# Beginning of a diffusion layer: lower halves of left blocks loaded in pairs, first high parts taken from PSUM, second tokens copied by two engines

## The chip, the cores and the metric

The kernel runs on one core of a Trainium2 chip. The metric is device time in microseconds (us) of one execution, lower is better; the figure given for a kernel is the median of several executions.

The core has five engines that run beside each other, each with its own queue of instructions in a fixed order: PE (TensorE, matrix products, with weight loads shown apart as PEld), DVE (VectorE), ACT (ScalarE), POOL (GpSimd) and SP (SyncE), which here only issues DMA transfers. They wait for each other through semaphores. Products are written to PSUM, a small memory that PE writes and that ACT and DVE read; everything else lies in SBUF, and inputs and outputs in HBM.

## The reference

One layer over 1024 latent tokens and 256 context tokens, width 1024, all in fp32: a SwiGLU FFN at half weight, a token mixer (gated short convolution beside grouped-query attention), a second FFN, and a final norm. Each part is normalised and modulated with a shift, a scale and a gate, made from the vector c.

```python
mod_lat = (jax.nn.silu(c) @ w_mod[layer] + b_mod[layer])[:, None, :]
ml = jnp.split(mod_lat, N_MOD, axis=-1)
x = x + 0.5 * ml[2] * swiglu(modulate(rms_norm(x, norm1_g), ml[0], ml[1]), ffn1_w_in, ffn1_w_out)
```

Only the start concerns us: the tokens x are read and normalised, `ml[1]` (scale) and `ml[0]` (shift) of the latents are made, and the first products of `ffn1_w_in` begin.

## The kernel before, in words

**Number format of the products.** An fp32 operand is split in two fp32r parts: a high part (a rounding cast) and a low part (the value minus the high part). A product is three matmuls: high by high, high by low, low by high. `split` does it with a cast on ACT and a subtraction on DVE.

**The products of the first FFN** go by a Winograd scheme (class `Winograd`): from the quarters of the weights and of the tokens seven products of half size are made for each of 22 column blocks, numbered 1 to 7 by the operand `r[i]` that they take. `r[1]` is the first half of the channels (0 to 511) of the first 512 tokens (C0), `r[2]` their second half (512 to 1023); `r[3]` to `r[7]` also need the second 512 tokens (C1). A product takes one left block (a weight tile of 128 by 512, in two parts) and is 12 matmuls of 128x512.

**The start by halves** (`start_by_half`, line 727). For the first `BY_HALF = 8` column blocks the products with `r[1]` are done first, which need only the upper halves of the blocks and the first half of the channels (left blocks 0 to 7; the first two products are interleaved). Then come the products with `r[2]`, with the lower halves (left blocks 8 to 15), each added by DVE to the result before. Five more column blocks follow with both products. `left()` keeps four left blocks ready: it draws from the generator `lefts` (line 618), which loads and splits. The upper halves come in pairs in tiles named `half`; each lower half has a buffer named `raw` to itself, of which there are three, each with room for two halves.

**What sets the order.** The instructions of each engine are ordered by a planner that plays the program through on modelled times: among the instructions that are ready it takes the one that stands earliest in the source, and it gives out the buffers of one kind in the source's order. Where the source says otherwise, an instruction is pinned: it comes after whatever stands just before it in the source for its engine. That is `pinned=True` for loads, matmuls and transposes, and `strict[0] = True` for all that is issued through `act`, `dve` and the others. The splits of the first 16 left blocks are pinned. The order is fixed before the run; on the chip an engine waits at an instruction whose inputs are late, and all behind it waits too.

**The modulation.** `first_mod` makes the first half of the scale (m = 1) on PE. `second_mod` (line 350) makes the others: DVE multiplies the rows of `w_mod` by silu(c) and sums them in `macc` (eight instructions, or four when `by_pe` is 4), the sum is split (`acch`, `accl`), PE adds over the partitions with a column of ones, ACT copies the row (`mrow`), PE turns it into a column, and DVE adds the bias into `modl`. `mod00` is the first half of the shift (m = 0); `mods1` is the second half of the scale, then of the shift, and its steps are drawn four at a time between the products of `start_by_half`.

**The tokens.** C0's tokens are scaled by their reciprocal norm (`scale_tokens`), then turned by PE (four transposes of 128x128 into a PSUM tile). The turned first half stays in four PSUM tiles `xh` until gain and shift are there; then `h0` is made (DVE for even k, ACT for odd k) and split by `keep` into `r[1]`. The second half is turned into `h0[k][:, 1]` once the first products are on their way, and later scaled, shifted and split into `r[2]`. C1's tokens are first turned unscaled by `turn_tokens` (eight times four transposes, one copy each; copies are for the residual), then scaled in place, and turned again in `norm1`, which makes `r[3]` to `r[7]` with sums and splits on DVE and ACT. `turn_tokens` takes PSUM tiles `pt` (two buffers) for even k and `po` (one buffer) for odd k.

Of the kernel before, what the change touches and what calls it, by code (L numbers as in the profile page):

```python
# [51 lines left out]
def tile_dit_layer(  # L52
# [56 lines left out]
    def uniq(s):  # L109
        n_tiles[0] += 1  # L110
        return f"{s}_{n_tiles[0]}"
# [238 lines left out]
    def second_mod(m, half, raws, by_pe=0):  # L350


        acc, nk = ttile("macc"), KD - by_pe
        for k in range(nk):
            raw, s = raws[k // 2][:, k % 2], silu_c[:, k : k + 1]
            if k:
                dve.scalar_tensor_tensor(out=acc, in0=raw, scalar=s, in1=acc, op0=ALU.mult, op1=ALU.add)
            else:
                dve.tensor_scalar(out=acc, in0=raw, scalar1=s, scalar2=None, op0=ALU.mult)
            yield  # L360
        ah, al = ttile("acch", dt=F32R), ttile("accl", dt=F32R)
        split(acc, ah, al)
        yield
        pr = ps_s()
        for k in range(nk, KD):
            raw, s = raws[k // 2][:, k % 2], silu_c[:, k : k + 1]
            matmul(pr[:1], s, raw, start=k == nk, stop=False, pinned=True)
            if k in (nk, KD - 1):
                yield
        matmul(pr[:1], ones_r[:], ah, start=not by_pe, stop=False)  # L370
        matmul(pr[:1], ones_r[:], al, start=False, stop=True)
        row = ttile("mrow")
        act.copy(out=row[:1], in_=pr[:1])
        yield
        pm = ps_t(4)
        for j in range(4):
            transpose(pm[:, j : j + 1], row[:1, j * P : (j + 1) * P])
        column_adds(m, half, pm, (0,))
        yield

# [111 lines left out]
    class Winograd:  # L492
# [21 lines left out]
        def keep(self, i, k, src, lo_eng=None):  # L514
# [3 lines left out]
            self.r[i][k] = t  # L518

        def modulated(self, out, k, ch, pr):  # L520
            dve.tensor_mul(out=out, in0=self.xs(k, ch), in1=pr)
            self.shifted(out, k)
# [95 lines left out]
        def lefts(self, pairs, side_from):  # L618
# [5 lines left out]

            def half_cols(src, half):
                t = wpool.tile([P, SLOT], F32, tag="raw", name=uniq("raw"), bufs=3)[:, :512]
                src = src[half * 512 : (half + 1) * 512]
                load(t.rearrange("p (k n) -> p k n", n=P), src.rearrange("(k p) n -> p k n", p=P))
                return t

# [11 lines left out]
            for t in self.halves[:m]:  # L642
                yield parts(t)
            for a, _ in pairs[:m]:
                yield parts(half_cols(a, 1))
            for a, _ in pairs[m:n]:
# [375 lines left out]

    def turn_tokens(ch, toks, engines=("dve", "act")):

        s, o, n = ch
        for k in range(KD):
            pt = (ps_o if k % 2 else ps_t)(n)
            for j, t in enumerate(toks):
                transpose(pt[:, j * P : (j + 1) * P], t[:, k * P : (k + 1) * P])
            dst = (xc if s == "c" else xs)(k, ch)  # L1030
# [54 lines left out]
    half1.h0 = h0 = [atile("h0", (P, 2, 512)) for _ in range(4)]  # L1085
    run(mod00, 1)
    half1.prefetch(2)
    run(mod00)
    for k in range(4):
        if k % 2:  # L1090
            half1.shifted(h0[k][:, 0], k, xh[k])
        else:
            dve.tensor_scalar(
                out=h0[k][:, 0], in0=xh[k], scalar1=gain1["l"][:, k : k + 1], scalar2=modl[:, k : k + 1],
                op0=ALU.mult, op1=ALU.add,
            )
        half1.keep(1, k, h0[k][:, 0])
    start = half1.start_by_half()
    run(start, 1)
    for k in range(4):  # L1100
        xt = turned(t0, k + 4, ps_o if k % 2 else ps_t)
        if k % 2:
# [3 lines left out]
    mods1 = (step for m, raws in ((1, raws11), (0, raws01)) for step in second_mod(m, 1, raws))  # L1106
    turn1 = turn_tokens(C1, t1, ("act", "act"))
    for j in range(2, BY_HALF):
        run(start, 1)
        run(mods1, 4)  # L1110
        if j == TOKENS_AT:
# [6 lines left out]
            run(turn1)  # L1118
            scale_tokens(t1, y1)
    run(mods1)  # L1120
# [780 lines left out]
```

## Time and profile before

| | us |
|---|---|
| median of 3 executions (lowest, highest) | 2656.81 (2656.78, 2657.75) |
| the profiled execution's own time | 2655.43 |
| its span, from the first instruction to the last | 2653.7 |
| PE busy | 2618.7 (99% of the span) |
| DVE busy | 2012.7 (76%) |
| ACT busy | 1172.7 (44%) |

The profile is of one execution. A time in a row is counted from the start of the span. A row of the order of time gives start, duration (of several: from the first's start to the last's end), engine, operation, out<-in with buffer numbers left out, and shapes; in square brackets stand the idle time of the engine before it and what ended it. The granted clock is the share of TensorE's full clock that PE was given. Names in rows: `ps`, `pt` and `po` are PSUM tiles, `wl` and `wh` the tiles of split left blocks (both hold a high and a low part), `r` the split token operands, `nt` the sums in `norm1`, `xtok` the tokens as loaded, `x` the turned tokens, `uc` the results of the start by halves.

### The profile page before, as it was taken

What the parts mean: (1) busy time and instruction counts of PE and PEld (TensorE: products, weight loads), DVE (VectorE), ACT (ScalarE), POOL (GpSimd) and SP (SyncE); (2) the same over time, 40 slices, a digit from 0 to 9 for tenths busy, and PEclk for the clock granted to TensorE, in tenths of its full rate; (3) what the DMA queues carried; (4) which work ended last, traced back from release to release, by engine and by line L of the source; (5) the groups of instructions that cost most, each with busy time, mean ns of one, the idle gap of its engine ahead of it and who ended that gap; (6) DMA issues with size and microseconds to landing.
All of it is one profiled execution on the core that took longest, in us unless ns stands there. A gap on an engine that the chain in (4) does not pass through costs nothing.

```text
span 2653.7 us, 35378 instructions
## 1 busy us (share of the span) xinstructions
PE 2618.7 (99%) x12665; PEld 2178.3 (82%) x12665; DVE 2012.7 (76%) x3382; ACT 1172.7 (44%) x2321; POOL 552.7 (21%) x425
## 2 busy tenths in 40 slices
PE   8999999999999999999999999999999999999998
PEld 5788799888788778888888888888887788888888
DVE  5778976887897899877798676685457876666996
ACT  6533354333454642333355576574235333334553
POOL 0143201112010044333023122141001442321100
PEclk9999999999999999999999999999999999999999
DMA  8556475344984355332522432113535552327831
GB/s 318 199 186 202 131 234 159 116 128 169 322 199 112 122 177 162 118 121 90 187 84 92 91 93 64 33 43 98 166 88 172 182 162 83 100 76 275 201 84 64
DMA packets 367017, 378.40 MB, mean 143 GB/s; under 512 B 19430, under 2 KB 252024, under 8 KB 366840
## 3 DMA queue, kind: packets, MB, share of 16 engines
q1 hardware_dynamic: 357400, 357.22, 41.7%
q0 software_dynamic: 9440, 18.91, 4.4%
q8 instruction: 99, 1.62, 0.3%
q14 instruction: 78, 0.64, 0.1%
HBM read 306.26 MB, written 69.76 MB: 142 GB/s over the span
## 4 chain that ended last, share of the span: by engine, by line
PE 85%; DVE 8%; DMA 2%; issue 2%; ACT 2%; POOL 0%; SPq 0%; DVEq 0%; ACTq 0%; POOLq 0%
PE ps L90 70%; PE po L90 8%; PE pt L90 7%; DVE wl L90 1%; DMA rawm<-in_w_mod_dram 1%; DVE u L90 1%; DVE macc L90 1%; DVE r L90 1%; DMA raw<-in_ffn_w_in_dram 1%; POOL sum L90 0%; DVE nt L90 0%; DVE y L90 0%; DVE xb L90 0%; DVE v L90 0%; DVE rs_t L90 0%
## 5 line engine op out<-in xcount | busy, mean ns | idle before, releaser
L90 PE MATMUL ps<-r,wl 128*128 128x512 f32 x5196 | 1208.7, 392 | 11.4 <-DVE wl L90 3.8
L90 PEld LDWEIGHTS ps<-r,wl 128*128 128x128 f32 x5196 | 974.9, 189 | 221.1 <-DVE wl L90 5.5
L90 ACT CAST wl<-raw 128x512 fp32r<-128x512 f32 x287 | 177.8, 620 | 222.4 <-PE ps L90 176.3
L90 ACT CAST wl<-sum 128x512 fp32r<-128x512 f32 x218 | 133.6, 620 | 305.9 <-PE ps L90 222.8
L90 DVE TENSOR_TENSOR wl<-raw,wl 128x512 fp32r<-128x512 f32 x287 | 204.3, 714 | 64.2 <-ACT wl L90 62.4
L90 DVE TENSOR_TENSOR wl<-sum,wl 128x512 fp32r<-128x512 f32 x218 | 198.3, 911 | 36.1 <-ACT wl L90 35.0
L90 POOL TENSOR_TENSOR sum<-raw 128x512 f32<-128x512 f32 x55 | 80.6, 1465 | 673.3 <-DMA raw<-in_ffn_w_in_dram 454.9
L90 DVE TENSOR_TENSOR u<-u,ps 128x512 f32<-128x512 f32 x186 | 126.3, 680 | 37.3 <-PE ps L90 37.3
L90 DVE SCALAR_TENSOR_TENSOR macc<-rawm,silu_c,macc 128x512 f32<-128x512 f32 x178 | 144.1, 827 | 13.4 <-DMA rawm<-in_w_mod_dram 12.9
L90 POOL TENSOR_TENSOR sum<-raw,sum 128x512 f32<-128x512 f32 x55 | 80.5, 1464 | 309.3 <-DVE wl L90 309.3
L90 ACT CAST rh<-hid 128x512 fp32r<-128x512 f32 x132 | 81.5, 621 | 136.5 <-PE ps L90 111.4
L90 DVE TENSOR_TENSOR pts<-pt,pts 128x512 fp32r<-128x512 f32 x160 | 108.8, 687 | 42.5 <-ACT pts L90 40.6
L90 ACT CAST pts<-pt 128x512 fp32r<-128x512 f32 x160 | 93.5, 595 | 86.4 <-PE pt L90 82.5
L90 DVE TENSOR_REDUCE m<-ps 128x1 f32<-128x512 f32 (+1 forms) x192 | 110.3, 595 | 23.9 <-PE ps L90 21.1
L90 PE MATMUL ps<-rh,wl 128*128 128x512 f32 x360 | 122.0, 389 | 0.0
L90 PE MATMUL ps<-wh,r 128*128 128x512 f32 x384 | 120.7, 392 | 0.0
L90 ACT CAST wh<-raw 128x512 fp32r<-128x512 f32 (+1 forms) x85 | 67.8, 801 | 101.9 <-PE ps L90 73.8
L90 DVE TENSOR_TENSOR rl<-hid,rh 128x512 fp32r<-128x512 f32 x132 | 90.4, 687 | 26.7 <-ACT rh L90 16.0
L90 PE MATMUL po<-pts,vh 128*128 128x512 f32 x256 | 110.0, 435 | 0.2 <-ACT pts L90 0.2
L90 PE MATMUL ps<-kl,qs 128*128 128x512 f32 x384 | 104.1, 395 | 0.0
L90 PE MATMUL ps<-rh,wh 128*128 128x512 f32 x300 | 102.3, 389 | 0.0
L90 PE MATMUL ps<-y,wc 128*128 128x512 f32 x384 | 97.1, 392 | 0.2 <-DVE g L90 0.2
(318 smaller groups left out, 5075.6 us busy)
## 6 DMA issues: line engine op xcount, KB each, us to landing
raw<-in_ffn_w_in_dram SPq DMA_DIRECT2D x130, 512.0 KB
raw<-in_ffn_w_out_dram SPq DMA_DIRECT2D x72, 512.0 KB
raw<-in_w_in_dram SPq DMA_DIRECT2D x61, 512.0 KB
rawm<-in_w_mod_dram SPq DMA_DIRECT2D x104, 256.0 KB
hid<-hd SPq DMA_DIRECT2D x40, 512.0 KB
rawm<-in_w_mod_dram SPq DMA_DIRECT2D x32, 512.0 KB
ucd<-uc SPq DMA_DIRECT2D x29, 512.0 KB
ws<-in_ffn_w_out_dram POOLq DMA_DIRECT2D x26, 512.0 KB, 6.4
```

The lines of the kernel that those rows point to most:

```text
L90: inst = getattr(self.engine, name)(*args, **kw)
```

## The change

1. **Modulation.** In `second_mod` the eight `macc` instructions of the scale's second half are pinned. For `mod00` the row copy and the add into `modl` are pinned, and the first two left blocks are drawn before `mod00`'s last two steps instead of between them; so their splits now stand before that row copy and that add.
2. **First token operand.** All instructions that make `h0`'s first half and `r[1]` are pinned. For even k the high part is no longer cast from `h0`: ACT computes it from the turned tokens in PSUM (`keep_turned`), with the same gain and shift; DVE still makes `h0` from the same PSUM tile and subtracts. The transposes of the second half are pinned, after the first two products.
3. **Lower halves.** Two lower halves go to one `raw` buffer, by two loads (`lower_halves`); left blocks 8 to 15 take four buffers instead of eight.
4. **Second tokens.** Of the eight copies of C1's turned tokens DVE takes those of odd k; before, ACT took all. Of the four tiles that are scaled in place ACT takes two; before, DVE took all.

```diff
@@ second_mod
+            strict[0] = not by_pe and m == 1
             if k:
                 dve.scalar_tensor_tensor(out=acc, in0=raw, scalar=s, in1=acc, op0=ALU.mult, op1=ALU.add)
             else:
                 dve.tensor_scalar(out=acc, in0=raw, scalar1=s, scalar2=None, op0=ALU.mult)
+            strict[0] = False
...
+        strict[0] = bool(by_pe)
         act.copy(out=row[:1], in_=pr[:1])
+        strict[0] = False
...
+        strict[0] = bool(by_pe)
         column_adds(m, half, pm, (0,))
+        strict[0] = False
@@ class Winograd
+        def keep_turned(self, i, k, turned, h):
+
+            t = atile(f"r{i}", (P, 2, 512), F32R)
+            self.shifted(t[:, 0], k, turned)
+            dve.tensor_sub(out=t[:, 1], in0=h, in1=t[:, 0].bitcast(F32))
+            self.r[i][k] = t
@@ lefts
-            def half_cols(src, half):
-                t = wpool.tile([P, SLOT], F32, tag="raw", name=uniq("raw"), bufs=3)[:, :512]
-                src = src[half * 512 : (half + 1) * 512]
-                load(t.rearrange("p (k n) -> p k n", n=P), src.rearrange("(k p) n -> p k n", p=P))
-                return t
+            def lower_halves(*srcs):
+                t = wpool.tile([P, 2, 512], F32, tag="raw", name=uniq("raw"), bufs=3)
+                for i, src in enumerate(srcs):
+                    load(t[:, i].rearrange("p (k n) -> p k n", n=P), src[512:].rearrange("(k p) n -> p k n", p=P))
+                return t[:, 0], t[:, 1]
...
-            for a, _ in pairs[:m]:
-                yield parts(half_cols(a, 1))
+            for j in range(0, m, 2):
+                yield from map(parts, lower_halves(pairs[j][0], pairs[j + 1][0]))
@@ the beginning
-    run(mod00, 1)
     half1.prefetch(2)
     run(mod00)
+    strict[0] = True
     for k in range(4):
         if k % 2:
             half1.shifted(h0[k][:, 0], k, xh[k])
+            half1.keep(1, k, h0[k][:, 0])
         else:
             dve.tensor_scalar(
...
-        half1.keep(1, k, h0[k][:, 0])
+            half1.keep_turned(1, k, xh[k], h0[k][:, 0])
+    strict[0] = False
...
-        xt = turned(t0, k + 4, ps_o if k % 2 else ps_t)
+        xt = turned(t0, k + 4, ps_o if k % 2 else ps_t, True)
...
-    turn1 = turn_tokens(C1, t1, ("act", "act"))
+    turn1 = turn_tokens(C1, t1, ("act", "dve"))
...
-            scale_tokens(t1, y1)
+            scale_tokens(t1, y1, True)
```

More of the change, by code (lines that the diff above doesn't have):

```diff
@@ L1021, in turned, with turn_tokens @@
         return pt
-    def turn_tokens(ch, toks, engines=("dve", "act")):
+    def turn_tokens(ch, toks, engines=("dve", "act"), pinned=False):
         s, o, n = ch
@@ L1028, in turn_tokens @@
             for j, t in enumerate(toks):
-                transpose(pt[:, j * P : (j + 1) * P], t[:, k * P : (k + 1) * P])
+                transpose(pt[:, j * P : (j + 1) * P], t[:, k * P : (k + 1) * P], pinned)
             dst = (xc if s == "c" else xs)(k, ch)
```

## The prediction

> **What bounds the kernel now.** I read the page first (its span), then the busy times by stretches of the beginning, then who waited for whom on PE up to 150 us, then the order of time on each engine around the waits. The change touches only work issued before about 110 us, so the stretches of the beginning count. In them the columns are busy us (instructions) of PE, PEld, DVE, ACT, POOL, then the granted clock, the DMA share and GB/s.
>
> ```profile
> span 2653.7 us, 35378 instructions
> 0.00:10.00 10.00, 6.38 (x36) 6.12 (x36) 0.24 (x2) 6.32 (x10) 0.71 (x6) 1.00 0.70 254
> 10.00:20.00 10.00, 9.79 (x44) 4.30 (x45) 6.43 (x20) 5.53 (x10) 0.00 (x0) 1.00 1.06 401
> 20.00:30.00 10.00, 8.38 (x41) 3.60 (x39) 6.00 (x14) 2.86 (x6) 0.00 (x0) 1.00 1.09 371
> 30.00:40.00 10.00, 8.90 (x38) 7.12 (x39) 9.96 (x16) 5.35 (x10) 0.00 (x0) 0.83 1.03 352
> 60.00:70.00 10.00, 7.52 (x38) 5.53 (x36) 6.87 (x14) 10.00 (x19) 0.00 (x0) 0.83 0.54 197
> 80.00:90.00 10.00, 10.00 (x54) 8.27 (x53) 10.00 (x18) 7.18 (x12) 0.00 (x0) 1.00 0.72 250
> 90.00:100.00 10.00, 7.71 (x29) 6.04 (x28) 9.98 (x18) 6.79 (x13) 0.00 (x0) 0.83 0.56 188
> ```
>
> PE is the bound nearly everywhere, except in three places: around 30, 63 and 91 us. In each it first waits, then runs with a granted clock of 0.83 over ten us, that is 1.7 us of full-speed work lost on top of the wait. The waits themselves, PE up to 150 us (total us, times, longest):
>
> ```profile
> PE ps L90 <- ACT wh L90: 2.3, 1, 2.3
> PE pt L90 <- ACT mrow L90: 1.4, 2, 0.7
> PE ps L90 <- ACT r L90: 1.3, 1, 1.3
> PE pt L90 <- DVE xtok L90: 1.2, 4, 0.5
> PE po L90 <- ACT x L90: 0.6, 1, 0.6
> PE pt L90 <- DVE h L90: 0.5, 1, 0.5
> ```
>
> Place 1 has half of the mrow wait, r and h: 0.7 + 1.3 + 0.5 = 2.5 us. Place 2 has the other half, xtok and x: 0.7 + 1.2 + 0.6 = 2.5 us. Place 3 is one wait of 2.3 us. With 1.7 us each for the clock, 7.3 + 5.1 = **12.4 us** is all that this change can reach; it will not clear three places at once.
>
> **The change part by part.** *Start of the first product (place 1).*
>
> ```profile
> 27.35 0.57 ACT L90 COPY mrow<-ps 1x512 f32<-1x512 f32 x1 [2.69 <-PE ps L90]
> 27.84 0.61 ACT L90 CAST wl<-half 128x512 fp32r<-128x512 f32 x1
> 28.42 0.16 DVE L90 TENSOR_TENSOR modl<-pt,bcol 128x4 f32<-128x4 f32 x1 [1.47 <-PE pt L90]
> 28.50 0.69 DVE L90 TENSOR_TENSOR wl<-half,wl 128x512 fp32r<-128x512 f32 x1
> 29.11 0.81 DVE L90 TENSOR_SCALAR h<-ps,gain_l,modl 128x512 f32<-128x512 f32 x1
> 29.95 0.62 ACT L90 CAST r<-h 128x512 fp32r<-128x512 f32 x1 [0.98 <-DVE h L90]
> 30.43 0.75 DVE L90 SCALAR_TENSOR_TENSOR macc<-rawm,silu_c,macc 128x512 f32<-128x512 f32 x1
> 30.47 0.77 ACT L90 ACTIVATE h<-ps,modl,gain_l 128x512 f32<-128x512 f32 x1
> 30.62 0.50 PE L90 MATMUL ps<-r,wl 128*128 128x512 f32 x1 [1.33 <-ACT r L90]
> 31.70 0.68 DVE L90 TENSOR_TENSOR r<-h,r 128x512 fp32r<-128x512 f32 x1
> 36.80 0.68 DVE L90 TENSOR_TENSOR r<-h,r 128x512 fp32r<-128x512 f32 x1
> ```
>
> Moved: the first two weights' casts and low parts now come before the mrow copy and the column add, into the 2.69 and 1.47 us in which ACT and DVE stood idle. So h starts where the low part started, 28.50 instead of 29.11. Added: h's high part goes from PSUM by ACT, 0.77 (the 30.47 row) instead of the cast's 0.62. No row shows ACT and DVE reading one PSUM tile side by side with neither needing the other. Bounds: side by side, the high part ends at 28.5 + 0.8 = 29.3 and PE starts 1.3 earlier; one after the other, it starts 0.84 after h (29.95 − 29.11), at 29.34, ends at 30.1, and PE starts at 30.15, 0.5 earlier. I take the second, as in the nearest row both engines read one PSUM tile and DVE's idle time is ended by ACT:
>
> ```profile
> L90 DVE TENSOR_TENSOR pts<-pt,pts 128x512 fp32r<-128x512 f32 x160 | 108.8, 687 | 42.5 <-ACT pts L90 40.6
> ```
>
> The Trainium skill speaks here against the change: "PSUM — Partial Sum Buffer", on bank collisions, says that two engines may not touch the same bank and partitions at once, two reads included, and that the compiler's scheduler puts a dependency between them. By it the sum is the one I took, 0.5; without it 1.3. No run here shows it yet.
>
> The low parts follow in written order with no macc (0.75, the 30.43 row) or copy between. From 30.15: low part 0 0.6; h 1 and its cast on ACT in 1.3, low part 1 0.6, ending at 32.0; h 2 and its high part one after the other 1.6, low part 2 beside h 3 and its cast 1.3, low part 3 0.7: 35.6. Before, low part 3 ended at 36.80 + 0.68 = 37.5. That is 1.9 earlier. Against it, the second half's 16 transposes are pinned behind the first 24 matmuls and no longer fill the waits; four take 0.44 on the chain, so 1.8 us come back later. And PE has even less to do up to 32 us, so the slow clock stays. Net: 0.5 us earlier, bounds −0.3 and 1.3.
>
> *Loads.*
>
> ```profile
> 12.71 4.56 SPq L90 DMA_DIRECT2D raw<-in_ffn_w_in_dram  x3
> 17.31 3.25 SPq L90 DMA_DIRECT2D half<-in_ffn_w_in_dram  x2
> ```
>
> Three raw buffers now take six loads, and up to three more may stand ahead of the first halves. What SP issued up to the halves is about 7.7 MB (4 + 8 loads of 0.52, 5 of 0.26, small ones); at 2.54 MB in the first ten us, 4.01 in the next and 371 GB/s after, the halves land by about 23. Three more (0.79 MB) make that 25.2, and the casts are done by 26.5 to 27, just ahead of 27.35. Cost 0, covered by that slack; without it the mrow copy queues behind them (bound 0.5 us). The gain of raw data earlier is judged at place 3.
>
> *Second half of the modulation, second tokens (place 2).*
>
> ```profile
> 47.19 0.48 DVE L90 TENSOR_SCALAR macc<-rawm,silu_c 128x512 f32<-128x512 f32 x1
> 48.65 0.57 ACT L90 COPY mrow<-ps 1x512 f32<-1x512 f32 x1
> 50.38 3.11 DVE L90 SCALAR_TENSOR_TENSOR macc<-rawm,silu_c,macc 128x512 f32<-128x512 f32 x4
> 59.66 0.61 ACT L90 COPY x<-po 128x512 f32<-128x512 f32 x1
> 62.53 2.93 ACT L90 ACTIVATE h<-h,modl,gain_l 128x512 f32<-128x512 f32 x4
> 63.04 2.74 DVE L90 TENSOR_SCALAR xtok<-xtok,rs_y 128x1024 f32<-128x1024 f32 x4 [0.72 <-PE po L90]
> 16.84 2.19 ACT L90 ACTIVATE xtok<-xtok,rs_y 128x1024 f32<-128x1024 f32 x2 [1.10 <-DVE rs_y L90]
> 67.03 0.78 PE L90 MATMUL ps<-r,wl 128*128 128x512 f32 x1
> 44.32 0.69 DVE L90 TENSOR_TENSOR wl<-half,wl 128x512 fp32r<-128x512 f32 x1 [1.33 <-ACT wl L90]
> ```
>
> Place 2 ends when r2 is there, and that hangs on the chain macc, mrow, modl, h. The scale's eight macc were spread over DVE's gaps from 25 to 40 us; now four are pinned behind the low parts of weights 4 and 5 and four behind that of weight 6, which was 44.32 and still follows product 2. So they end no sooner than 45.0 + 4 × 0.78 = 48.1; cast 0.6, low part 0.7 and two row matmuls 0.8 put the first mrow at 50.2, against 48.65. The shift's eight macc begin around that copy (47.19 before), so **1.6 us later**, or 3.5 if PE takes a whole product (2.7) first. From 47.19 to 62.53 are 15.3 us, of which the chain's own work is 0.5 + 7 × 0.75, 0.6, 0.7, 0.8, 0.6 and about 0.6 for turn and add: 8.5. The other 7 are queues, mostly ACT's, which is full (10.00 in 60 to 70). There four of the eight copies (0.6 each, 2.4) go to DVE, and two scalings (2.19) come, but only when all turns are done, so partly while ACT waits for this chain. I put the relief at 1.6, which cancels the delay: product(2) begins at **67.0**, bounds 64.5 and 70. The 0.5 of the start only lengthens this wait.
>
> *Place 3.*
>
> ```profile
> 88.04 0.62 ACT L90 CAST wl<-raw 128x512 fp32r<-128x512 f32 x1 [1.65 <-DMA raw<-in_ffn_w_in_dram]
> 91.53 0.62 ACT L90 CAST r<-nt 128x512 fp32r<-128x512 f32 x1 [0.16 <-DVE nt L90]
> 92.05 0.61 ACT L90 CAST wh<-raw 128x512 fp32r<-128x512 f32 x1
> ```
>
> PE waits for the cast at 92.05, the last of the lower halves. It is not late for its data: it is pinned behind the cast at 91.53, that one came right after DVE's nt, and DVE is full (10.00 and 9.98). Raw data loaded earlier takes the 1.65 us at 88.04 away, but that idle time stands beside a full DVE: worth 0. What helps is DVE: scaling on it falls from 2.74 to 1.4, the scaled tokens are ready some us sooner, and nt and r work can start in the 3.1 us in which DVE stood idle from 60 to 70. I put the cast 1 to 3 us earlier, and of 2.3 + 1.7 at this place I take half, **2.0** (bounds 0 and 4.0).
>
> **Sum:** 0 + 0 + 0 − 2.0, from the profiled execution's own 2655.43 (its span of 2653.7 and 1.7 around it): 2653.4. The median shown is 1.4 above that execution, so **2654.8** by the median, 0.08% less. What this kernel's times can tell from no change is put at 0.2%, 5.3 us.
>
> **The rivals.** *B, two places clear:* the high part is read side by side, ACT's relief beats the pins, product(2) begins 2.5 earlier and place 3 goes whole (4.0): 2656.8 − 6.5 = **2650.3**. For it speaks that ACT has not a gap from 60 to 70; against it, that the pins delay the chain ahead of ACT. The clock could add to it: the rows give 0.83 after waits of which the longest are 1.3, 0.7 and 2.3. The Trainium skill, "TensorE: Matmul & The Clock Gate", Part 1, has half rate only after a whole idle window of some 3.4 us; by that rule shortened waits would surely keep the clock and I would give B 0.4. The rows show the slow clock after shorter waits, so the trace does not agree. *C, hidden:* DVE stays the bound of place 3 whatever comes earlier, and nothing else shows: **2656.8**. For it: 9.98 and 10.00. *D, slower, a new wait in place 2:* the row matmuls of the scale slip behind one more product (2.7), y1's steps and four copies compete with the shift's macc on DVE, and r2 comes at 71.2, 4.2 later, with place 3 as before: **2661.0**. It decides from the point where the shift's first macc begins after 52 us. Against it: DVE had 3.1 us free in 60 to 70.
>
> **How the numbers follow.** Forecast 0.43 (2652 to 2657), B 0.27, C 0.15, D 0.15. Range 2648.5 to 2661: B's with the clock of one more place kept (1.7) to D's; about 0.1 lies below and 0.08 above. Faster by over 5.3 us (below 2651.5): most of B and a little of the forecast, 0.27. Slower by over 5.3 (above 2662.1): the part of D in which two products slip ahead, 0.07. The rest, 0.66.
>
> **What would show it.** Start: h about 0.6 earlier; ACT's high part beginning after DVE's h (my sum) or with it (B). Loads: no idle time of ACT before the mrow copy that a half's DMA ends. Place 2: first macc of the shift at 49 to 51, product(2) near 67. Place 3: PE's wait there under 2.3 us with DVE full. I am wrong if product(2) moves by more than 3 us, if place 3's cast waits for its load, or if the stretches after 130 us change by more than 1 us in sum.

## The result, and the profile after

The changed kernel is **slower**: 2672.73 us (median of 6 runs, 2671.22 to 2673.9) against 2656.8 for the kernel before beside it (6 runs, 2651.17 to 2657.97), ratio 1.0063 [1.0053, 1.0073]. 2654.8 was forecast, so the time missed is some 18 us. The profiled execution took 2672.8 us.

First the stretches of the profile after, columns as in the prediction: busy us (instructions) of PE, PEld, DVE, ACT and POOL, granted clock, DMA share, GB/s.

```profile
30.00:40.00 10.00, 9.37 (x35) 7.61 (x36) 5.02 (x8) 6.06 (x10) 0.00 (x0) 0.71 1.08 369
...
50.00:60.00 10.00, 5.15 (x16) 3.84 (x15) 7.46 (x11) 1.21 (x2) 0.00 (x0) 0.66 0.36 138
...
70.00:80.00 10.00, 5.17 (x27) 3.41 (x27) 5.71 (x17) 8.08 (x13) 0.00 (x0) 0.83 0.38 147
...
100.00:110.00 10.00, 7.15 (x31) 5.59 (x30) 10.00 (x18) 6.08 (x11) 0.00 (x0) 0.87 0.51 191
...
130.00:2600.00 2470.00, 2453.80 (x11731) 2041.07 (x11730) 1881.59 (x3113) 1078.20 (x2150) 545.37 (x417) 1.00 0.46 139
```

The same view of the kernel before, where its rows are not yet shown:

```profile
50.00:60.00 10.00, 10.00 (x58) 8.08 (x58) 7.74 (x21) 8.20 (x16) 0.00 (x0) 1.00 0.51 176
...
130.00:2590.00 2460.00, 2443.66 (x11698) 2034.79 (x11697) 1883.56 (x3107) 1074.76 (x2143) 541.35 (x411) 1.00 0.46 138
```

After 130 us nothing changed: PE stands still for 16.2 us of 2470 there, and for 16.3 of 2460 before. All is lost in the beginning, and the largest part of it in a stretch that before had no gap at all: 50 to 60 us, where PE is now busy for 5.15 us, at 0.66 of its clock. If the work lost in ten us is taken as ten less busy time times clock, the stretches up to 130 us add up to 15.4 us before and 29.3 after. The 13.9 more lie thus: 1.6 from 0 to 40 us, 6.9 from 40 to 60, 4.8 from 60 to 90, 0.6 from 90 to 130. This is rough, since the clock is a mean over each row; the spans, 2671.0 and 2653.7, differ by 17.3.

Who PE waited for from 20 to 150 us after the change (total us, times, longest):

```profile
PE ps L90 <- ACT acch L90: 4.8, 1, 4.8
PE ps L90 <- ACT wh L90: 2.9, 1, 2.9
```

The greatest wait is new: PE waits for `acch`, the high part of the scale's sum. The order of time on PE, ACT and DVE shows how it comes about and what it leaves behind (start, duration, engine, operation, out<-in, idle time before and what ended it):

```profile
44.94 0.60 PE L90 MATMUL po<-ident,xtok 128*128 128x128 f32 x4
45.57 0.59 ACT L90 COPY h<-po 128x512 f32<-128x512 f32 x1 [2.12 <-PE po L90]
46.71 0.69 DVE L90 TENSOR_TENSOR wl<-half,wl 128x512 fp32r<-128x512 f32 x1 [5.47 <-ACT wl L90]
47.92 0.48 DVE L90 TENSOR_SCALAR macc<-rawm,silu_c 128x512 f32<-128x512 f32 x1
51.28 3.11 DVE L90 SCALAR_TENSOR_TENSOR macc<-rawm,silu_c,macc 128x512 f32<-128x512 f32 x4
54.42 0.62 ACT L90 CAST acch<-macc 128x512 fp32r<-128x512 f32 x1 [3.77 <-DVE macc L90]
55.09 0.59 PE L90 MATMUL ps<-acch,ones_r 128*1 128x512 f32 x1 [4.85 <-ACT acch L90]
55.48 4.85 PE L90 MATMUL ps<-r,wh 128*128 128x512 f32 x12
55.68 0.48 DVE L90 TENSOR_SCALAR macc<-rawm,silu_c 128x512 f32<-128x512 f32 x1
61.77 0.40 PE L90 MATMUL ps<-accl,ones_r 128*1 128x512 f32 x1
63.14 0.56 ACT L90 COPY mrow<-ps 1x512 f32<-1x512 f32 x1
63.60 0.61 ACT L90 CAST wl<-raw 128x512 fp32r<-128x512 f32 x1
64.25 0.69 DVE L90 TENSOR_TENSOR wl<-raw,wl 128x512 fp32r<-128x512 f32 x1 [6.51 <-ACT wl L90]
80.00 0.80 PE L90 MATMUL ps<-r,wl 128*128 128x512 f32 x1 [0.59 <-ACT r L90]
```

The same view of the kernel before, for the same steps:

```profile
39.95 0.59 ACT L90 COPY h<-po 128x512 f32<-128x512 f32 x1 [2.68 <-PE po L90]
41.09 0.69 DVE L90 TENSOR_TENSOR wl<-half,wl 128x512 fp32r<-128x512 f32 x1 [0.95 <-ACT wl L90]
41.48 0.62 ACT L90 CAST acch<-macc 128x512 fp32r<-128x512 f32 x1
47.97 0.40 PE L90 MATMUL ps<-acch,ones_r 128*1 128x512 f32 x1
```

It is a ring of three engines, each with a fixed order. The last four transposes for the first tokens stand behind products on PE (44.94). ACT waits for them to copy `h`, with the cast of the next weight, at 46.05, behind that copy. DVE waits 5.47 us for that cast, and the pinned `macc` stand behind its low part. So the scale's sum begins at 47.92, where before its high part had been ready since 42.1, 5.9 us ahead of its use at 47.97. Now PE's order has come to the sum's first row matmul long before the sum is there: it waits 4.85 us, and the next 12 matmuls take 4.85 us, 0.40 each instead of 0.23.

A second round follows. The order has the low part's row matmul 19 matmuls behind the high part's, so on the slow clock it comes at 61.77. ACT copies the row at 63.14 (48.65 before), with the cast of the first whole weight behind it, and DVE waits 6.51 us for that cast, in the middle of the shift's sum. The shift is late, and with it `r[2]`: product(2) starts at 80.00 instead of 67.03.

### The profile page after: what moved, and what is told of

It is laid out like the page before. It is cut to its first block, busy times and chain, and to the rows that moved or that the text cites. A ratio compares the mean times of both kernels' runs of the same rounds, so it can differ in the third digit from the quotient of the medians.

```text
span 2671.0 us, 35369 instructions
## 1 busy us (share of the span) xinstructions
PE 2627.1 (98%) x12665; PEld 2182.0 (82%) x12665; DVE 2008.3 (75%) x3384; ACT 1174.3 (44%) x2319; POOL 549.3 (21%) x425
## 4 chain that ended last, share of the span: by engine, by line
PE 59%; DVE 2%; ACT 1%; issue 1%; POOL 0%; DMA 0%; SPq 0%; DVEq 0%; ACTq 0%; POOLq 0%
PE ps L90 49%; PE po L90 5%; PE pt L90 5%; DVE xb L90 0%; DVE y L90 0%; DVE r L90 0%; POOL sum L90 0%; DMA raw<-in_w_in_dram 0%; DVE wl L90 0%; SPq L90 0%; DVE rs_t L90 0%; ACT r L90 0%; DVE wc L90 0%; ACT pts L90 0%; DVE pts L90 0%
```

## The experiments

In the list the ratio is to the kernel before beside it, whose median was 2654.89 to 2656.8. Differences in us below are between medians; where the ratios give another number by more than 1 us, both stand. "By 150 us" is how many matmuls of PE the profile shows up to then; as the rest is alike, it tells roughly how far PE is behind. Before it is 643, after 580: 63 matmuls, at 0.227 us each 14 us.

| kernel | median us | ratio [95%] | by 150 us |
|---|---|---|---|
| after | 2672.73 | 1.0063 [1.0053, 1.0073] | 580 |
| no_macc_pin | 2659.12 | 1.0015 [1.0005, 1.0024] | 631 |
| no_turn_pin | 2663.45 | 1.0026 [1.0015, 1.0036] | 618 |
| no_both_pins | 2656.42 | 1.0002 [0.9993, 1.0012] | 646 |
| before_macc_pin | 2657.17 | 1.0007 [0.9997, 1.0016] | 634 |
| sum_ahead | 2674.62 | 1.0074 [1.0058, 1.0089] | 572 |
| before_sums_ahead | 2669.71 | 1.0053 [1.0041, 1.0066] | 590 |
| rows_swapped | 2663.89 | 1.0039 [1.0025, 1.0053] | 609 |
| rows_later | 2665.86 | 1.0042 [1.0028, 1.0056] | 604 |
| rows_later_together | 2662.63 | 1.0026 [1.0015, 1.0037] | 621 |
| high_from_sbuf | 2670.29 | 1.0056 [1.0042, 1.0069] | 586 |
| single_loads | 2671.08 | 1.0063 [1.0047, 1.0078] | 589 |
| before_second_tokens | 2655.26 | 0.9998 [0.9989, 1.0007] | 648 |
| tokens_and_order | 2653.55 | 0.9995 [0.9987, 1.0004] | 650 |
| late_casts_free | 2658.30 | 1.0010 [1.0001, 1.0019] | 642 |
| lower_casts_free | 2654.44 | 1.0000 [0.9991, 1.0008] | 654 |

### Which pin: four kernels around two pins

`no_macc_pin` is the kernel after without the pin on the scale's `macc`:

```diff
-            strict[0] = not by_pe and m == 1
...
-            strict[0] = False
             yield
```

> The changed kernel with one part undone: the multiply-adds of the scale's second half are no longer pinned. Theory 'pinned sums': the sum over raw weights runs late because it is held behind the low parts of weights 4 to 6 (47.9 to 54.3 us after the change, 25.7 to 40.1 before), and the row matmul that PE's order holds at 50 us waits 4.8 us for it. Without the pin the sum ends by 40 us, the 4.8 us wait is gone, product(2) begins at 66 to 69 us and the time is 2654 to 2659. Theory 'turned block': the pinned transposes of the first tokens' second half hold ScalarE's copies until 45.6 us and with them the casts of weights 4 and 5; this edit leaves them so, and at least 8 of the 16 us stay: 2664 or more.

`no_turn_pin` is the kernel after without the pin on the 16 transposes of the second half:

```diff
-        xt = turned(t0, k + 4, ps_o if k % 2 else ps_t, True)
+        xt = turned(t0, k + 4, ps_o if k % 2 else ps_t)
```

> The changed kernel with another part undone: the 16 transposes of the first tokens' second half are no longer pinned behind the first 24 matmuls. 'Pinned sums': the casts of weight 4 come some 4 us earlier, the scale's sum ends at about 50 instead of 54.3 us, the row matmul's wait shrinks from 4.8 to about 1 us, but the shift's sum still stands behind the first low part of a whole weight (64.3 us): product(2) at 73 to 78 us, 2662 to 2670. 'Turned block': the copies and casts are back where they were, and so is the time: 2654 to 2660.

`no_both_pins` has both edits:

> The changed kernel with both parts undone, the pin of the scale's sum and the pin of the transposes. 'Pinned sums': as without the first alone, 2653 to 2658, the transposes worth under 2 us. 'Turned block': as without the second alone. If this one is still over 2662, neither is the cause and another part of the change is (the first high parts from PSUM, the paired loads, the second tokens' copies).

`before_macc_pin` is the kernel before with the `macc` pin alone:

```diff
+            strict[0] = not by_pe and m == 1
...
+            strict[0] = False
             yield
```

> The kernel before with one part added: the multiply-adds of the scale's second half are pinned. 'Pinned sums': the sum, 25.7 to 40.1 us before, comes behind the low part of weight 4 and later (about 42.5 to 49 us), the shift's sum follows in the same way, and the time rises to 2662 or more with product(2) at 73 us or later. 'Turned block': the transposes run early here, the casts are not held, so the pin costs under 4 us: 2655 to 2660.

Without both pins the loss is gone: 0.6 us against before, nothing that can be told from zero. So the rest of the change (pinned start, high parts from PSUM, paired loads, second tokens on two engines) together costs and brings nothing that shows, to within some 3 us. With the transposes' pin alone (`no_macc_pin`) the loss is 3.3 us, with the `macc` pin alone (`no_turn_pin`) 7.6, with both 16. Together they cost 5 to 6 us more than the sum of the two; each of the three losses is known to about 2.6 us either way. `no_turn_pin` and `no_both_pins` fell where 'pinned sums' had put them and `no_macc_pin` 0.1 us beside it, but `before_macc_pin` fell where only the rival, 'turned block', had put it. The row matmul of `no_turn_pin`, in order of time, and the low part that its `macc` stand behind:

```profile
42.20 0.69 DVE L90 TENSOR_TENSOR wl<-half,wl 128x512 fp32r<-128x512 f32 x1 [4.62 <-ACT wl L90]
50.59 0.59 PE L90 MATMUL ps<-acch,ones_r 128*1 128x512 f32 x1 [3.13 <-ACT acch L90]
```

and the same low part, the row matmul and place 3 of `before_macc_pin`:

```profile
38.37 0.69 DVE L90 TENSOR_TENSOR wl<-half,wl 128x512 fp32r<-128x512 f32 x1 [0.85 <-ACT wl L90]
...
47.96 0.40 PE L90 MATMUL ps<-acch,ones_r 128*1 128x512 f32 x1 [0.86 <-ACT acch L90]
...
94.97 0.72 PE L90 MATMUL ps<-r,wh 128*128 128x512 f32 x2 [0.42 <-ACT wh L90]
```

In the kernel before, the `macc` pin uses up the 5.9 us and leaves a wait of 0.86. Product(2) is later there too (71.92), but PE then comes later to place 3 and waits there for 0.42 instead of 2.3, which gives most of it back: the time is up by 1.3 us, which its interval does not tell from zero. In the change's own surroundings the same pin stands behind a low part that comes 3.8 us later (42.20 against 38.37), and the wait is 3.13. With the transposes pinned as well the low part comes at 46.71, and the wait is 4.85. The two pins draw on the same slack.

### Is it the pin, or the place of the row matmul?

If the sum were only late because DVE gets to it late, drawing its steps ahead of the loop should cure it. `sum_ahead` does that to the kernel after, `before_sums_ahead` to the kernel before:

```diff
+    run(mods1, 8)
     for j in range(2, BY_HALF):
         run(start, 1)
         run(mods1, 4)
```

> The changed kernel, every part kept, both pins too; only the scale's eight multiply-adds are drawn before the loop over the products instead of four at a time inside it, so that they are pinned behind the low parts of weights 2 and 3 and not of 4 to 6. Theory 'ring' (the two pins together cost 16 us because ScalarE waits for the pinned transposes, its casts of weights 4 to 6 wait behind, the low parts wait for the casts, the pinned sum for the low parts, and PE for the sum): the sum runs from about 41 to 47 us, the row matmul's wait falls from 4.8 to at most 2.5 us, the shift's sum is over by 58, product(2) begins at 60 to 68 us, 2652 to 2660. Theory 'any pin' (a fixed place of the sum costs by itself, wherever it is): product(2) after 74 us, 2664 or more.

> The kernel before with the modulation's steps drawn one block earlier (eight steps ahead of the loop), nothing else. 'Ring': what sets the start of product(2) is the chain from the shift's sum to r2; the shift's row is read some 10 us earlier (52 instead of 61.1 us), r2 is there by 62 us, product(2) begins at 58 to 63 us without place 2's waits (2.5 us and 1.7 us of clock), 2650 to 2653. Rival 'given back': PE comes to place 3 sooner and waits there the longer, since VectorE is the bound there: place 3's wait rises from 2.3 to 5 us or more and the time is 2655 to 2658.

In both the theory 'ring' failed. `sum_ahead` alone could still be read as its rival, 'any pin', which had said 2664 or more. `before_sums_ahead` rules that out: the kernel before, with no pin of the change in it, becomes 13.9 us slower. Its order of time:

```profile
54.83 0.49 PE L90 MATMUL ps<-acch,ones_r 128*1 128x512 f32 x1 [3.29 <-ACT acch L90]
55.12 4.42 PE L90 MATMUL ps<-r,wl 128*128 128x512 f32 x12
61.42 0.40 PE L90 MATMUL ps<-accl,ones_r 128*1 128x512 f32 x1
```

It is the picture of the change, at the *shift's* sum: PE waits for `acch`, goes on at half speed, and the second row matmul stands 21 matmuls on. (PE also waits 2.91 us for a copy `x` at 66.82 there, so not all of the 13.9 us hangs on the row matmul.) `sum_ahead` has the same wait for the shift's `acch`, 3.62 us, at 61.87. The extra steps drew forward not only the sums but also the row matmuls in PE's order, ahead of what DVE can do. So the theory that the pinned `macc` as such cost the time fell. What the runs share is a row matmul whose place in PE's order comes before its sum is there. The pins do that by moving the sum back, the extra steps by moving the row matmul forward.

### What the wait leaves behind: the pair of row matmuls

The next three take the kernel after and leave both pins. `rows_swapped` has the low part's row matmul first, so that the two stay together:

```diff
-        matmul(pr[:1], ones_r[:], ah, start=not by_pe, stop=False)
-        matmul(pr[:1], ones_r[:], al, start=False, stop=True)
+        matmul(pr[:1], ones_r[:], al, start=not by_pe, stop=False)
+        matmul(pr[:1], ones_r[:], ah, start=False, stop=True)
```

> The changed kernel; only the two row matmuls of each sum change places (low part first). In PE's order both then stand together, in front of the product with weight 5, where the high part's alone stood; the order leaves no 19 matmuls between them any more. So PE waits for the scale's sum as long as before or longer (4.8 to 6 us at 50 us), but the row copy and, behind it on ScalarE, the cast of the first whole weight come at 56 to 58 instead of 63.1 to 63.6 us, VectorE's idle 6.5 us in the middle of the shift's sum are gone and that sum ends by 64 instead of 69.5. Theory 'chain' (most of the 16 us is the shift's sum coming late): product(2) at 73 to 76 instead of 80 us, 2664 to 2668. Theory 'stall' (most of it is PE's wait at the row matmul and the slow clock behind it): 2670 or more.

`rows_later` gives the scale's row matmuls four empty steps, so that they come one product later:

```diff
         split(acc, ah, al)
         yield
+        for _ in range(0 if by_pe or m == 0 else 4):
+            yield
         pr = ps_s()
```

> The changed kernel; only four empty steps are put between the scale's split and its row matmuls, so that these are drawn one product later. In PE's order they then stand behind the product with weight 5 (12 matmuls, 2.7 us), and on ScalarE the cast of the first whole weight stands before the row copy. 'Stall': PE's wait falls from 4.8 to at most 2.2 us and with it goes some of the slow clock; 'chain': the shift's sum has no gap in it and product(2) begins at 72 to 76 us. By both, 2660 to 2667. If it is over 2669, neither the place of the row matmuls nor the gap explains the loss.

`rows_later_together` has both:

> The changed kernel with both edits on the row matmuls: they change places, and are drawn one product later. Both pins stay. PE's order then has both rows behind the product with weight 5 and VectorE's shift sum has neither the cast of a whole weight nor the add into modl to wait for. 'Chain and stall together': PE waits 2.5 to 3.5 us for the scale's sum instead of 4.8, the shift's sum ends by 62 (69.5 in the changed kernel, 62.8 with the rows only swapped), product(2) begins at 72 to 75 us, and the time is 2658 to 2663. If it is above 2665, the two shares do not add up and a third loss is left among the pins.

`rows_swapped` in order of time:

```profile
55.38 0.59 PE L90 MATMUL ps<-accl,ones_r 128*1 128x512 f32 x1 [5.58 <-DVE accl L90]
56.42 0.57 ACT L90 COPY mrow<-ps 1x512 f32<-1x512 f32 x1 [1.83 <-PE ps L90]
58.16 4.68 DVE L90 SCALAR_TENSOR_TENSOR macc<-rawm,silu_c,macc 128x512 f32<-128x512 f32 x6
76.53 0.79 PE L90 MATMUL ps<-r,wl 128*128 128x512 f32 x1
```

PE's wait is no shorter than it was (5.58 us), yet the kernel is faster than after by 8.8 us (6.4 by the ratios): the row is copied 6.7 us sooner, DVE makes the shift's sum without a break, and product(2) is 3.5 us earlier. So some 40 to 55% of the loss is not the wait but the low part's row matmul left behind; the time fell just below what 'chain' had said, 2664 to 2668. `rows_later` in order of time:

```profile
54.48 0.39 PE L90 MATMUL ps<-acch,ones_r 128*1 128x512 f32 x1 [2.34 <-ACT acch L90]
61.09 0.40 PE L90 MATMUL ps<-accl,ones_r 128*1 128x512 f32 x1
71.40 0.40 PE L90 MATMUL ps<-acch,ones_r 128*1 128x512 f32 x1 [3.52 <-ACT acch L90]
```

Here the wait is halved (2.34) and the pair still apart, and PE waits a second time, 3.52 us, for the shift's sum, and 2.63 us more for `h` at 79.42; it is 6.9 us faster than after (5.6 by the ratios). The time is in the range expected, but product(2) is not: it is even later than after, 81.04. Yet in its profile the stretch from 100 to 110 us has PE busy for 9.92 at full clock, where after the change it was 7.15 at 0.87. Both together, in order of time:

```profile
55.95 0.39 PE L90 MATMUL ps<-accl,ones_r 128*1 128x512 f32 x1 [3.07 <-DVE accl L90]
...
74.67 0.79 PE L90 MATMUL ps<-r,wl 128*128 128x512 f32 x1 [1.95 <-ACT r L90]
```

Together they give 10.1 us (9.8 by the ratios), less than the sum of the two, 15.7 (12.0). What is left, 7 to 8 us, is still a wait of 3.07, one of 1.95, product(2) 7.6 us late, and 0.52 of the clock from 70 to 80 us. How the rest divides among these was not settled.

### The start and the loads

`high_from_sbuf` is the kernel after with all its pins, but with the even high parts cast from `h0` again:

```diff
-            half1.keep_turned(1, k, xh[k], h0[k][:, 0])
+            half1.keep(1, k, h0[k][:, 0])
```

> The changed kernel with only the first high parts undone: for even k the high part is cast from h0 again, not computed from PSUM. 'Ring': the chain through the transposes is as it was, 2668 to 2676; the start of the first product moves by 0.2 us at most, since ScalarE read the PSUM tile only after VectorE (h ends 29.77, high part begins 29.80 us), and 0.78 against 0.62 us is all that the two ways differ by. Theory 'second reader' (the tile po that both engines read is free later, and the transposes, the copies and the casts come later for that): the row matmul's wait falls under 3 us and the time under 2665.

`single_loads` is the kernel after with a `raw` buffer for each lower half again:

```diff
-            for j in range(0, m, 2):
-                yield from map(parts, lower_halves(pairs[j][0], pairs[j + 1][0]))
+            for a, _ in pairs[:m]:
+                yield parts(half_cols(a, 1))
```

> The changed kernel with only the paired loads undone: each lower half has a raw buffer to itself again. My step 'Loads' put the pairs at 0: if so, 2671 to 2674. If the three more loads ahead of the halves cost the start something (the trace of the changed kernel has ScalarE waiting 2.4 us for a half's transfer until 26.5 us, 0.35 us later than the row copy stood before), the casts of the halves start by 25.5 and the first product 0.3 to 1 us earlier, and the time falls by as much, since everything behind hangs on the same order: 2670 to 2673.

The start in the kernel after, in order of time:

```profile
26.47 0.62 ACT L90 CAST wl<-half 128x512 fp32r<-128x512 f32 x1 [2.44 <-DMA half<-in_ffn_w_in_dram]
27.70 0.57 ACT L90 COPY mrow<-ps 1x512 f32<-1x512 f32 x1
28.96 0.81 DVE L90 TENSOR_SCALAR h<-ps,gain_l,modl 128x512 f32<-128x512 f32 x1
29.80 0.78 ACT L90 ACTIVATE r<-ps,modl,gain_l 128x512 fp32r<-128x512 f32 x1 [1.54 <-DVE h L90]
30.63 0.80 PE L90 MATMUL ps<-r,wl 128*128 128x512 f32 x1 [1.91 <-ACT r L90]
```

ACT's high part waits until DVE has done `h` from the same PSUM tile (29.77; the profile lets DVE's `h` end the wait), though neither needs the other's result. In `high_from_sbuf`, where the cast reads `h0` itself, it begins at 30.15, after an `h` that ends at 30.12: the same gap. Taking the high part from PSUM saves no waiting then, and costs 0.78 instead of 0.62. `high_from_sbuf` is 2.4 us faster than after, with intervals that overlap.

In `single_loads` the first halves are cast earlier:

```profile
24.80 0.61 ACT L90 CAST wl<-half 128x512 fp32r<-128x512 f32 x1
...
27.59 0.57 ACT L90 COPY mrow<-ps 1x512 f32<-1x512 f32 x1 [1.65 <-PE ps L90]
```

So the pairs do delay the first halves, by at least 1.7 us. In the profile after, PE's row was ready at 26.69 and its copy waited 1.0 us behind the two casts; here the casts are out of the way, but the row itself was ready only at 27.56, so that the copy comes 0.1 earlier. By the whole time the pairs cost nothing that shows: the ratio is that of after, 1.0063.

### Place 3

`before_second_tokens` is the kernel before with the change's fourth part alone:

```diff
-    turn1 = turn_tokens(C1, t1, ("act", "act"))
+    turn1 = turn_tokens(C1, t1, ("act", "dve"))
...
-            scale_tokens(t1, y1)
+            scale_tokens(t1, y1, True)
```

> The kernel before with only the part on the second tokens: VectorE takes four of the eight copies, ScalarE two of the four scalings. My prediction's step for place 3: its wait of 2.3 us falls to about 1 us or its slow clock goes, product(2) begins at 65.5 to 67.5 us, 2653 to 2655. Rival 'hidden': place 3 stays at 2 us or more and the time is within 1 us of before. Rival 'later r2': VectorE's four copies stand before r2's low parts, or ScalarE's two scalings (2.2 us) before r2's casts, product(2) begins after 68 us: 2657 or more.

`tokens_and_order` also pins the steps that make `r[2]` in the order of the source:

```diff
+    strict[0] = True
     for k in range(4):
         half1.shifted(h0[k][:, 1], k + 4)
         half1.keep(2, k, h0[k][:, 1])
+    strict[0] = False
```

> The kernel before with the part on the second tokens, and the making of r2 (shift, cast, shift, cast) pinned in written order instead of all shifts first. Looks for a version better than both. If place 2 hangs on the first of r2's casts, product(2) begins at 65 to 67 us instead of 67.6 and the time is 2651 to 2654; if ScalarE's scalings of the second tokens and the casts of weights hold it as before, or the products with r2 now wait for its later parts, 2655 to 2660.

Two more loosen the pin on the splits of the lower halves on top of that, `late_casts_free` for left blocks 13 to 15 and `lower_casts_free` for 8 to 15:

```diff
-                strict[0] = bool(self.side_from) and self.n_left <= 2 * BY_HALF
+                strict[0] = bool(self.side_from) and self.n_left <= 2 * BY_HALF - 3
```

```diff
-                strict[0] = bool(self.side_from) and self.n_left <= 2 * BY_HALF
+                strict[0] = bool(self.side_from) and self.n_left <= BY_HALF
```

> The kernel before with the part on the second tokens and r2 made in written order, and in addition the splits of the left blocks 13 to 15 not pinned. With place 2 shortened, place 3 had its wait of 2.6 us again, for the cast of left block 15, pinned behind casts that wait for VectorE's sums; free, that cast stands in front of them in ScalarE's order. If the pin is what holds it, place 3's wait is under 1 us and the time 2649 to 2652.5; if its raw data or another cast comes last, 2653 to 2656.

> As the one before, with the splits of all eight lower halves (left blocks 8 to 15) not pinned. Casts then come as early as their raw data lands. Place 3's wait goes as with the last three alone, if the pin holds it; but early casts now stand on ScalarE in front of the turned second tokens' copies and r2's shifts, which may put product(2) later than 66 us: 2649 to 2657.

`before_second_tokens`, the wait at place 3 and the cast that it is for, in order of time:

```profile
92.03 0.62 ACT L90 CAST wh<-raw 128x512 fp32r<-128x512 f32 x1
92.70 0.73 PE L90 MATMUL ps<-r,wh 128*128 128x512 f32 x2 [0.59 <-ACT wh L90]
```

Its stretches of places 2 and 3:

```profile
60.00:70.00 10.00, 6.65 (x34) 4.80 (x33) 6.06 (x16) 9.79 (x16) 0.00 (x0) 0.83 0.54 193
90.00:100.00 10.00, 8.76 (x42) 6.96 (x41) 9.87 (x18) 6.08 (x11) 0.00 (x0) 1.00 0.57 196
```

By the wait alone, place 3 does what was forecast of it: PE waits for the lower half's cast for 0.59 instead of 2.3, the clock stays at 1.00 (0.83 before), and busy time rises from 7.71 to 8.76. But the cast itself, forecast 1 to 3 us earlier, begins at 92.03, where before it began at 92.05. The wait is shorter because PE comes later: product(2) begins at 68.12 (67.03 before), after a wait of 1.47 us for ACT's scaled tokens at 66.05, and from 60 to 70 us PE is busy for 6.65 instead of 7.52. The whole is 0.6 us faster, within the interval, as the rival 'hidden' had it. What held the cast shows in one more row of the kernel before, ahead of the cast at 91.53 of which the prediction speaks:

```profile
90.75 0.62 ACT L90 CAST wl<-raw 128x512 fp32r<-128x512 f32 x1 [1.40 <-DMA raw<-in_ffn_w_in_dram]
```

This cast stood idle for its load until 90.75 and ended at 91.37, and `nt` was ready 0.16 us later. So two things held the cast of place 3, the load and DVE's `nt`, and doing away with one of them alone gains 0.16 us at most. In `before_second_tokens` that load was there sooner, its cast at 89.03, but ACT's next instruction waited 1.20 us for PE's `po`, until 90.84, and PE was late.

With `r[2]` in order, place 2 gets better (product(2) at 65.20; 8.43 busy from 60 to 70), and PE waits longer again at place 3. That row of `tokens_and_order`, in order of time (the profiled executions of this kernel and of `late_casts_free` were the slowest of eleven each, so their rows tell where PE waits rather than how much it costs in the median):

```profile
91.60 1.22 PE L90 MATMUL ps<-r,wh 128*128 128x512 f32 x2 [2.58 <-ACT wh L90]
```

With the late casts free that wait is gone (90 to 100 us: 10.00 at full clock), and a longer one stands 17 us on, in `late_casts_free`:

```profile
108.34 5.49 PE L90 MATMUL ps<-r,wh 128*128 128x512 f32 x12 [3.96 <-ACT uc L90]
```

and a shorter one in `lower_casts_free`:

```profile
108.21 3.02 PE L90 MATMUL ps<-r,wh 128*128 128x512 f32 x12 [1.50 <-ACT uc L90]
```

So the pin on the late casts does hold up place 3. The expectation had it behind casts that wait for DVE's sums; in `tokens_and_order` ACT's idle time ahead of the cast was ended by loads (3.60 us at 88.39, 0.87 at 89.89). In `late_casts_free` the corresponding pair of loads is also issued sooner, at 81.87 and 83.07 instead of from 84.16 on. How the gain divides between casts and loads was not tested. Clearing this place handed a wait on to the next fixed point, and `late_casts_free` missed both of its ranges. None of the kernels is measurably faster than before; the best median, 2653.55, has an interval that holds 1.

## Why the prediction was wrong

**What bounds the kernel, and the 12.4 us to be had.** The reading of the three places stands in so far as each is a wait and a slow clock. But the prediction looked only for places where PE already waited. The dearest place after the change, 55 us, was one where PE had never waited, and its slack (`acch` ready at 42.1, used at 47.97) was in the trace and was not read.

**Start: +0.5 forecast, 0 measured.** The choice was right: ACT's high part began behind DVE's `h`, 0.03 us after its end, not beside it. The Trainium skill's rule, "PSUM — Partial Sum Buffer", on bank collisions, agrees with 29.77 and 29.80. The row given for the choice, `pts<-pt,pts`, does not bear it out: there DVE reads ACT's result, and so must wait for it. But `h` began at 28.96 and not at 28.50: the row copy came 0.35 later than before, behind the casts of the late halves, and `h` stood 0.2 us behind `modl` instead of 0.1. The first product came at 30.63 (30.62 before), the last low part was done at 36.20 (35.6 forecast, 37.5 before), and the slow clock did not only stay, as said: it was 0.95 and 0.71 from 20 to 40 us, where it had been 1.00 and 0.83.

**Loads: halves forecast by 25.2 at the latest.** They were cast at 26.47, right after landing, and ACT's idle time was ended by them, which the prediction had named as a sign against it. The slack that was to cover them, 27.35, was not there: the row was ready at 26.69, and its copy waited 1.0 us, twice the bound of 0.5. The gain of the start went into that.

**Second half of the modulation: the step that failed.** The prediction had the scale's `macc` "end no sooner than 45.0 + 4 × 0.78 = 48.1", the first row copied at 50.2, and the shift's sum "1.6 us later". Measured: the scale's `macc` ended at 54.4, the row was copied at 63.14, the shift's first `macc` came at 55.68 (8.5 later) and product(2) at 80.00 (13.0 later; 67.0 forecast). Two things in that step were wrong.

First, it took the low part of weight 6 at its time in the kernel before, 44.32; after the change it came at 50.67. The change itself moves what stands ahead of it: the pinned transposes hold ACT's copy of `h`, and the casts of weights 4 to 6 stand behind that copy. The prediction priced that pin only as "1.8 us come back later", on PE, and did not follow the transposes' result to ACT and from there to DVE. `no_turn_pin` against after shows the size: the first low part of the row, that of weight 4, at 42.20 against 46.71, and 9.3 us of the time.

Second, it gave the two row matmuls 0.8 us, as if PE would take them when the sum is ready. Their place is fixed. PE came to the first, waited 4.85 us, lost some 2 us more at the slow clock, and had 19 matmuls ahead of the second. `rows_swapped` shows the worth of that last part: 6 to 9 us.

The gain of 1.6 that was to cancel the delay, ACT's relief by DVE, could not show in this kernel; alone, in `before_second_tokens`, it made place 2 worse (6.65 busy against 7.52, product(2) 1.1 us later).

Two sums of this step do not come out either. The chain's own work as listed adds up to 9.05 us, not 8.5, which leaves 6.3 for queues; and 1.6 with a whole product of 2.7 makes 4.3, not 3.5. Neither changes the forecast of 67.0.

**Place 3: 2.0 forecast, none measured.** The reading "It is not late for its data" was half of the matter: the cast ahead of the two had waited for its load until 90.75, so that the load, put at "worth 0", and DVE's `nt` held the place to within 0.16 us of each other. Alone, in `before_second_tokens`, the step made the cast 0.02 us earlier instead of 1 to 3. That the wait fell below 2.3 there, the sign named for the step, was luck: PE was late. After the change PE waits there for the lower half's cast too, 2.85 us, at 107.0. The sign named for an error, a cast waiting for its load, did not come there: the cast stands behind one that waits 3.21 us for DVE's `nt`, with DVE full (10.00 from 100 to 110).

**The rivals.** B and C did not come as times, though C's picture of place 3, nothing earlier there, is what `before_second_tokens` showed. D had the sign and the place right (the row matmuls and the shift's sum), and its point of decision, a first `macc` of the shift after 52 us, was passed at 55.68. It was priced at 4.2 us later for product(2), with products slipping in ahead and no wait of PE itself; that is a third of the 13.0. "Two products slip ahead" was the right picture for the second row matmul, and it was given 0.07.

**After 130 us** nothing was to change, and nothing did.

## What to carry to other kernels

The price of pinning an instruction is not its own work but the slack between when its result is ready and the fixed place of its first user on another engine; read both times for each pin, and follow the result around the ring of engines until it comes back. Two pins can draw on the same slack and cost more together than one by one: here 3.3 and 7.6 us made 16, and one of them put into the kernel before cost 1.3. And take what stands ahead of a moved step at its time *after* the change, since the change's other parts move it. A wait that gets shorter is no proof of a gain: look whether what is waited for comes earlier, or only the one who waits later.

## What the runs showed of the hardware

- **The clock after a single wait.** Waits of 2.0 us and more in the midst of full work were followed by a slow clock: 2.03 (`before_sums_ahead`, at 104.86; 0.55 and 0.60 in the stretches of 2 us from 106 on), 2.3 (before, place 3, 0.83 over the ten us), 3.96 (`late_casts_free`, 12 matmuls in 5.49 us), 4.85 (after, 12 in 4.85). Waits of 0.59 (`before_second_tokens`) and 1.50 (`lower_casts_free`, 12 matmuls in 3.02 us) were not. A wait of 4.85 us thus costs about 7: 12 matmuls at full speed take 2.7 to 2.9.
- **How long it stays slow.** In stretches of 2 us the clock falls to 0.50. If a stretch between 0.50 and 1.00 is taken as part slow and part full, the slow time adds up to 3.4 us after the waits of 2.3 (before), 2.34 (`rows_later`) and 2.85 (after), and to 6.8 after those of 3.13 (`no_turn_pin`), 3.96 and 4.85. After 3.07 and 3.29 it was 3.4 again (`rows_later_together`, `before_sums_ahead`). After a wait of 2.3 that is 1.7 us of full-speed work; after one of 4.85 a part of the slow time lies in the wait itself.
- **Several short waits** can do it as well: at the start, 1.63 and 1.91 us (after) were followed by a slow clock until 35.8. The Trainium skill, "TensorE: Matmul & The Clock Gate", Part 1, gives half rate after a whole idle window of some 3.4 us; the wait of 2.3 at place 3 is shorter, so the trace does not bear that out as it stands. What exactly is counted was not tested.
- **Two readers of one PSUM tile.** ACT's read began 0.03 us after DVE's had ended, although it needed none of DVE's result. The profile shows it waiting for that instruction, with the same 0.03 us as where ACT does need the result (30.15 after 30.12); so it is a dependency of the program, and what two reads side by side would do no run here shows.
